# Moving copies and scalings of a mixer from VectorE to ScalarE and GpSimd in a two-layer hybrid model

## The chip, the core and the metric

The kernel runs on one core of a Trainium2 chip. The core has five engines that run beside each other and meet only at semaphores: TensorE (PE) multiplies matrices into PSUM, VectorE (DVE) and ScalarE (ACT) work elementwise on SBUF and PSUM, GpSimd (POOL) works elementwise on SBUF, and SyncE (SP) starts the transfers. Each engine takes its instructions in the order in which they stand in its queue. The metric is the device time of one execution in microseconds.

## The reference

Two layers, each made of a SwiGLU feed-forward block, a mixer, a cross attention and a second feed-forward block, with a layer norm behind each. There are 256 tokens of width 1024, everything in float32. The mixer is what matters here. It projects the tokens into a gated short convolution, a gated linear recurrence of four heads (hgrn2) and a pool over windows of 2, 4, 8 and 16 tokens:

```python
def hgrn2(q, f_logit, v, g, lb, norm_g):
    f = lb + (1.0 - lb) * jax.nn.sigmoid(f_logit.astype(f32))
    logf = jnp.log(f)
    k = 1.0 - f
    ...
        decay = jnp.exp(jnp.where(mask[:, :, None], diff, -jnp.inf))
        attn = jnp.einsum('bhtd,bhsd,bhtsd->bhts', qb, kb, decay)
        o = (jnp.einsum('bhts,bhsv->bhtv', attn, vb)
             + jnp.einsum('bhtd,bhdv->bhtv', qb * jnp.exp(b), state))
    ...
    o = o * lax.rsqrt(jnp.mean(jnp.square(o), axis=-1, keepdims=True) + RMS_EPS)
    o = o * norm_g.reshape(REC_HEADS, REC_HEAD_DIM).astype(f32)
    o = o.reshape(bsz, s, REC_DIM) * jax.nn.sigmoid(g.astype(f32))
```

The pool's group sums are multiplied by a small matrix and by a scale per channel (`y * scale`). The three results, side by side, go through `w_out`.

## The kernel before, in words

Every weight is loaded once from HBM in raw blocks of 1 MB. A helper `split` (L61, L62) turns each half of a block into two parts: ACT casts it to a rounded float (`whi`, L61), and DVE subtracts that from the raw value (`wlo`, L62). Large products run as three products of such parts (L100 to L103) and share one line, L103. PSUM tiles come from two rings of four, `acc` and `dn`; a product that needs a tile of a ring waits until the reader of the tile four places earlier is done.

A product's result leaves PSUM by two steps: ACT copies one half (L123, or L599 in the forward form used here), and DVE adds the other half to it (L124, or L600 and L601).

The mixer works on two blocks of 128 tokens. It computes the recurrence without a scan, by levels: at level c (1, 2, 4, ..., 64) the products of q and k between neighbouring blocks of c tokens are taken (L672) and written into the matrix `AT` under a mask (`copy_predicated`, L698). Between levels, q and k are multiplied in place by the decay across the block (L691 for q, L688 for k). The products at a level need the k of every second block in contiguous order, so `blocks(c)` (L657 to L663) copies them into a tile `kc`, of which there are two; the copy is on line 660 and, before, on DVE. The copy for level 2c reads what L688 of level c wrote, and L688 of level 2c writes over what the copy read.

The order of the PE in this part is written out by hand (`manual_schedule` with PE): between the products of the levels stand the projections of the values, the pool, the convolution and the gates. After the last level comes the product across the two token blocks (L715, copied out on ACT at L716). Then, for each of the two token blocks i: the products with v (L726, L727), the squares with their row sums on ACT (L731, four heads), the mean plus epsilon (L732), the power -0.5 on POOL (L733), the scaling of the result into `yr` (L734), and gate 1 + i (`gate`, with L599 to L601; every second gate is followed by the sigmoid at L612 on ACT and a scaling at L614 on DVE). Gate 3 comes after the loop. Behind it stand the pool's small product (L767) and its scaling (L770), the splits of the convolution and the pool into `xT`, the transposes of `yr` (L778), the first product with `w_out`, and, from `fill`, products of keys for the attention that do not depend on the mixer.

The order on the other engines is set by a scheduler that places the instructions when the program is built; it follows from the dependencies and the engine each instruction is on. A changed engine can therefore change the order of its neighbours.

Of the kernel before, what the change touches and what calls it, by code (L numbers as in the profile page):

```python
# [11 lines left out]
AF = mybir.ActivationFunctionType  # L12
ALU = mybir.AluOpType
# [4 lines left out]
P = 128  # L18
# [6 lines left out]
HEADS = 4  # L25
ALPHA = (2.0 * DEPTH) ** 0.25
LN_EPS = 1e-5
RMS_EPS = 1e-6
# [18 lines left out]
def model(ctx: ExitStack, tc: tile.TileContext, t: dict, out: bass.AP):  # L47
    nc = tc.nc
# [5 lines left out]
    def acc(shape=(P, 2, SEQ), tag="acc"):  # L54
        return ps.tile(list(shape), F32, tag=tag, name=tag)
# [138 lines left out]
    psc = prm[:, 28:32].rearrange("p (l j) -> p l j", l=DEPTH)  # L194
# [351 lines left out]
    def mixer(l, fill):  # L546
        w_in = t["w_in"][l]
        with tc.tile_pool(name="mix", bufs=1, reuse_waits="tile") as mp:
# [90 lines left out]
            def view(x, base, *dims, keep=False):  # L639
                return bass.AP(  # L640
                    tensor=x.tensor, offset=x.offset + base,
                    ap=[list(x.ap[0])] + [list(d) for d in dims if keep or d[1] > 1],
                )

            other = HEADS * P
            for b in range(NT):
                o = acc((P, HEADS, P), "dn")
# [9 lines left out]
            def blocks(c):  # L657

                kc = mp.tile([P, HEADS, P], F32, tag="kc", name="kc", bufs=2)
                nc.vector.tensor_copy(  # L660
                    kc.rearrange("p h (a w c) -> p w (h a) c", w=2, c=c),
                    view(kf, 0, (other + c, 2), (2 * c, HEADS * 64 // c), (1, c), keep=True),
                )  # L663
                return kc

            kc = blocks(1)
            for n, c in enumerate(LEVELS):
                a = 64 // c
                products_of_others((1, 2, 1, 2, 1, 2, 2)[n])
                o = acc((P, HEADS, NT, 64), "dn")  # L670
# [18 lines left out]
                if c < 64:  # L689
                    kc = blocks(2 * c)  # L690
# [16 lines left out]
            def gate(j, o=None):  # L707
                add_forward(sg[:, j, :], mm_cols(w_gate, slice(j * P, (j + 1) * P), xT) if o is None else o)
                if j % 2:
                    ev_g(j // 2)  # L710

            first = mm_cols(w_gate, slice(0, P), xT)
            o = acc((P, HEADS, P), "dn")
# [6 lines left out]
            yr = mp.tile([P, NT, HEADS, P], F32, tag="f", name="yr")  # L720
            for i in range(NT):
                o = acc((P, HEADS, P), "dn")
                for hh in range(HEADS):
                    c = slice(hh * P, hh * P + P)
                    if i:
                        nc.tensor.matmul(o[:, hh, :], AX_[:, hh, :], v[:, 0, c], start=True, stop=False)  # L726
                    nc.tensor.matmul(o[:, hh, :], AT[:, i, hh, :], v[:, i, c], start=i == 0, stop=True)  # L727
                ss = sm.tile([P, HEADS], F32, tag="ss", name="ss")
                jk = mp.tile([P, P], F32, tag="jk", name="jk", bufs=2)
                for hh in range(HEADS):  # L730
                    nc.scalar.activation(jk, o[:, hh, :], AF.Square, accum_out=ss[:, hh : hh + 1])  # L731
                nc.vector.tensor_scalar(ss, ss, 1.0 / P, RMS_EPS, op0=ALU.mult, op1=ALU.add)  # L732
                nc.gpsimd.tensor_tensor(ss, ss, nhalf, op=ALU.pow)  # L733
                nc.vector.tensor_tensor(yr[:, i], o, ss[:, :, None].to_broadcast([P, HEADS, P]), op=ALU.mult)  # L734
                gate(1 + i)
            gate(3)
            by_hand.__exit__(None, None, None)
# [3 lines left out]
            for g, w_ in enumerate(WINDOWS):  # L741
# [4 lines left out]
                    op=ALU.add,  # L746
                )
                pr, j = slice((g % 2) * 64, (g % 2) * 64 + 64), g // 2
# [7 lines left out]
            for j in range(2):  # L756
                nc.vector.tensor_scalar_mul(yc[:, j, :], u[:, j, 2 : 2 + SEQ], cw[:, l, 2, j : j + 1])
                for s in (1, 0):
                    nc.vector.scalar_tensor_tensor(  # L759
                        yc[:, j, :], u[:, j, s : s + SEQ], cw[:, l, s, j : j + 1], yc[:, j, :],  # L760
                        op0=ALU.mult, op1=ALU.add,
# [3 lines left out]
            o = acc()  # L765
            for j in range(2):
                nc.tensor.matmul(o[:, j, :], wpool[:, l, j, :], win[:, j, :], start=True, stop=True)  # L767
            yp = win
            for j in range(2):
                nc.vector.tensor_scalar_mul(yp[:, j, :], o[:, j, :], psc[:, l, j : j + 1])  # L770


            split(xTh[:, 0:2, :], xTl[:, 0:2, :], yc)
# [102 lines left out]
    for l in range(DEPTH):  # L876
        pend = ffn(l, "ffn1", 0, pend, early=None if l else lambda op: (load_memory(op), small_parameters(op)))
        keys(l, 0, {6: pend})
        pend = mixer(l, lambda: keys(l, 1))
        pend = attention(l, pend)  # L880
        pend = ffn(l, "ffn2", 3, pend, last=l == DEPTH - 1)
# [27 lines left out]
```

## Time and profile before

| | |
|---|---|
| median of 3 runs | 1117.33 us (1117.31 to 1117.41) |
| the profiled execution | 1118.65 us |
| its span, first to last instruction | 1116.9 us |
| granted TensorE clock, mean | 0.998 |
| PE, DVE, ACT, POOL busy | 1102.9, 822.4, 594.2, 41.8 us |
| first mixer's levels and end | about 213 to 277 us |
| second mixer's levels and end | about 763 to 827 us |

A row of a time line gives the start of an instruction from the start of the span, its length, its engine, its source line, its operation, what it writes and reads, and how many like it follow each other; in brackets stands how long the engine was idle before it and who ended that. A row of a group gives the count, the busy time, the mean length in nanoseconds and the idle time before. Several instructions on an engine overlap at their ends, so the distance between starts is shorter than a length.

### The profile page before, as it was taken

What the parts mean: (1) busy time and instruction counts of PE and PEld (TensorE: products, weight loads), DVE (VectorE), ACT (ScalarE), POOL (GpSimd) and SP (SyncE); (2) the same over time, 40 slices, a digit from 0 to 9 for tenths busy, and PEclk for the clock granted to TensorE, in tenths of its full rate; (3) what the DMA queues carried; (4) which work ended last, traced back from release to release, by engine and by line L of the source; (5) the groups of instructions that cost most, each with busy time, mean ns of one, the idle gap of its engine ahead of it and who ended that gap; (6) DMA issues with size and microseconds to landing.
All of it is one profiled execution on the core that took longest, in us unless ns stands there. A gap on an engine that the chain in (4) does not pass through costs nothing. (4 is left out here: it accounts for less than half of the span.)

```text
span 1116.9 us, 15747 instructions
## 1 busy us (share of the span) xinstructions
PE 1102.9 (99%) x6227; PEld 992.6 (89%) x6227; DVE 822.4 (74%) x1195; ACT 594.2 (53%) x873; POOL 41.8 (4%) x80
## 2 busy tenths in 40 slices
PE   9999999999999999999999999999999999999997
PEld 7989998998889889999889999889988998999996
DVE  6766677898888666666677666598988777766665
ACT  6665553645466456455355555455454653665550
POOL 7000000000000000000000000000000000000000
PEclk9999999999999999999999999999999999999999
DMA  8855565743465375656466655655445645755551
GB/s 309 301 211 202 194 221 156 240 170 139 163 243 180 105 262 191 226 204 211 151 226 234 214 182 186 237 186 194 151 146 183 237 152 164 249 189 203 181 182 38
DMA packets 98378, 218.23 MB, mean 195 GB/s; under 512 B 3776, under 2 KB 16352, under 8 KB 98304
## 3 DMA queue, kind: packets, MB, share of 16 engines
q1 hardware_dynamic: 97536, 215.89, 56.1%
q8 instruction: 49, 0.80, 0.3%
q10 hardware_dynamic: 576, 1.18, 0.3%
q14 instruction: 25, 0.20, 0.1%
q0 software_dynamic: 192, 0.15, 0.0%
HBM read 216.15 MB, written 1.05 MB: 194 GB/s over the span
## 5 line engine op out<-in xcount | busy, mean ns | idle before, releaser
L62 DVE TENSOR_TENSOR wlo<-raw,whi 128x1024 fp32r<-128x1024 f32 (+1 forms) x396 | 469.1, 1208 | 102.6 <-ACT whi L61 66.6
L61 ACT CAST whi<-raw 128x1024 fp32r<-128x1024 f32 (+1 forms) x396 | 398.2, 1041 | 170.7 <-PE dn L103 127.6
L103 PE MATMUL acc<-xT,whi 128*128 128x512 f32 x1600 | 388.3, 381 | 0.6 <-DVE xT L62 0.6
L103 PEld LDWEIGHTS acc<-xT,whi 128*128 128x128 f32 x1600 | 288.9, 190 | 33.8 <-DVE xT L62 1.1
L103 PEld LDWEIGHTS acc<-xT,wlo 128*128 128x128 f32 x1600 | 209.7, 191 | 10.8
L103 PE MATMUL acc<-xT,wlo 128*128 128x256 f32 x1600 | 210.8, 275 | 0.0
L103 PE MATMUL dn<-whi,ah 128*128 128x512 f32 x346 | 131.6, 380 | 0.0
L103 PE MATMUL dn<-wlo,ah 128*128 128x512 f32 x346 | 131.1, 379 | 0.0
L103 PE MATMUL dn<-whi,al 128*128 128x512 f32 x346 | 131.1, 379 | 0.0
L103 PE MATMUL dn<-whi,xT 128*128 128x512 f32 x288 | 88.9, 384 | 0.0
L103 PE MATMUL acc<-whi,xT 128*128 128x512 f32 x288 | 88.4, 381 | 0.0
L124 DVE TENSOR_TENSOR sg<-acc,sg 128x256 f32<-128x256 f32 x72 | 30.4, 422 | 69.7 <-ACT sg L123 69.6
L103 PEld LDWEIGHTS dn<-whi,al 128*128 128x128 f32 x346 | 65.4, 189 | 9.3
L103 PEld LDWEIGHTS dn<-wlo,ah 128*128 128x128 f32 x346 | 65.4, 189 | 9.2
L103 PEld LDWEIGHTS dn<-whi,ah 128*128 128x128 f32 x346 | 65.5, 189 | 8.6
L123 ACT COPY sg<-acc 128x256 f32<-128x256 f32 x72 | 26.7, 371 | 84.0 <-PE acc L103 83.8
L103 PEld LDWEIGHTS dn<-whi,xT 128*128 128x128 f32 x288 | 54.8, 191 | 7.5
L103 PEld LDWEIGHTS acc<-whi,xT 128*128 128x128 f32 x288 | 54.3, 189 | 7.6
L103 PE MATMUL dn<-wlo,xT 128*128 128x512 f32 x144 | 54.9, 381 | 0.0
L103 PE MATMUL acc<-wlo,xT 128*128 128x512 f32 x144 | 54.6, 379 | 0.0
L123 ACT COPY up<-acc 128x256 f32<-128x256 f32 x72 | 26.7, 370 | 49.0 <-PE acc L103 48.0
L304 POOL TENSOR_TENSOR rs<-rs,nhalf 128x1 f32<-128x1 f32 x16 | 14.9, 933 | 903.6 <-DVE rs L303 903.6
(196 smaller groups left out, 1048.5 us busy)
## 6 DMA issues: line engine op xcount, KB each, us to landing
raw<-in_ffn_up_dram SPq DMA_DIRECT2D x44, 1024.0 KB, 5.1
raw<-in_ffn_down_dram SPq DMA_DIRECT2D x44, 1024.0 KB, 4.9
raw<-in_ffn_gate_dram SPq DMA_DIRECT2D x42, 1024.0 KB, 5.0
raw<-in_w_in_dram SPq DMA_DIRECT2D x24, 1024.0 KB, 5.1
raw<-in_ca_k_dram SPq DMA_DIRECT2D x8, 1024.0 KB, 5.0
raw<-in_w_out_dram SPq DMA_DIRECT2D x8, 1024.0 KB, 4.9
raw<-in_ca_v_dram SPq DMA_DIRECT2D x8, 1024.0 KB, 6.0
raw<-in_ca_q_dram SPq DMA_DIRECT2D x8, 1024.0 KB, 5.0
```

The costliest lines, as they stand in the source:

```text
L61: nc.scalar.copy(hi, src)
L62: nc.vector.tensor_tensor(lo, src, hi.bitcast(F32), op=ALU.subtract)
L103: nc.tensor.matmul(o, w, x, start=start, stop=stop)
L123: nc.scalar.copy(dst, o[:, 1])
L124: nc.vector.tensor_tensor(dst, o[:, 0], dst, op=ALU.add)
L304: nc.gpsimd.tensor_tensor(rs, rs, nhalf[:, 0:1], op=ALU.pow)
```

## The change

Four edits, all in the mixer, none of which changes a product on the PE or a transfer:

1. The copy of the blocks of k into `kc` (seven per layer) is an ACT copy instead of a DVE copy.
2. The multiplication by 1/128 and the addition of epsilon on the sums of squares (two per layer, 128x4) is on POOL instead of DVE, directly ahead of the power that was there already.
3. The scaling of the recurrence's result into `yr` (two per layer) becomes four ACT activations each, one per head, whose scale is that head's column of `ss`.
4. The scaling of the pool's two sums (two per layer) becomes ACT activations with a column as the scale.

```diff
@@ blocks(c)
-                nc.vector.tensor_copy(
+                nc.scalar.copy(
                     kc.rearrange("p h (a w c) -> p w (h a) c", w=2, c=c),
                     view(kf, 0, (other + c, 2), (2 * c, HEADS * 64 // c), (1, c), keep=True),
                 )
@@ the loop over the token blocks
                     nc.scalar.activation(jk, o[:, hh, :], AF.Square, accum_out=ss[:, hh : hh + 1])
-                nc.vector.tensor_scalar(ss, ss, 1.0 / P, RMS_EPS, op0=ALU.mult, op1=ALU.add)
+                nc.gpsimd.tensor_scalar(ss, ss, 1.0 / P, RMS_EPS, op0=ALU.mult, op1=ALU.add)
                 nc.gpsimd.tensor_tensor(ss, ss, nhalf, op=ALU.pow)
-                nc.vector.tensor_tensor(yr[:, i], o, ss[:, :, None].to_broadcast([P, HEADS, P]), op=ALU.mult)
+                for hh in range(HEADS):
+                    nc.scalar.activation(yr[:, i, hh, :], o[:, hh, :], AF.Copy, scale=ss[:, hh : hh + 1])
                 gate(1 + i)
@@ the pool
             for j in range(2):
-                nc.vector.tensor_scalar_mul(yp[:, j, :], o[:, j, :], psc[:, l, j : j + 1])
+                nc.scalar.activation(yp[:, j, :], o[:, j, :], AF.Copy, scale=psc[:, l, j : j + 1])
```

As built, the PE's and SP's orders are the same as before. On ACT, the four scalings of token block i stand directly behind the squares of that block and ahead of the half copy of gate 1 + i; behind the second of these half copies follow two weight casts, the cast of the convolution into `xT`, the half copy of gate 3, another weight cast and the two scalings of the pool. On DVE the two weight remainders still stand between the evictions of gates 2 and 3.

## The prediction

> **What bounds the kernel now.** I read the page's head first, then the PE's waits, then three stretches of the first mixer, then the time lines of PE, DVE, ACT and POOL where the PE stands still.
>
> ```profile
> span 1116.9 us, 15747 instructions
> PE 1102.9 (99%) x6227; PEld 992.6 (89%) x6227; DVE 822.4 (74%) x1195; ACT 594.2 (53%) x873; POOL 41.8 (4%) x80
> ```
> ```profile
> PE acc L103 <- DVE sg L601: 2.4, 2, 1.2
> PE dn L389 <- DVE kTh L384: 1.5, 1, 1.5
> PE dn L715 <- DVE q L691: 1.2, 2, 0.6
> ```
> ```profile
> 222.00:261.00 39.00, 38.83 (x247) 35.67 (x245) 38.79 (x76) 16.16 (x23) 0.00 (x0) 1.00 0.47 161
> 261.00:277.00 16.00, 14.36 (x96) 13.24 (x97) 12.42 (x31) 10.21 (x29) 2.20 (x2) 1.00 0.37 132
> ```
> TensorE is busy for 99% of the span, so a change on other engines can only move its waits. In the mixer there are two kinds, once per layer: 0.6 us at L715 for the last rescaling of q on DVE, and 1.2 us at the first product of the keys behind the mixer, for the DVE copy of the last gate (L601), which frees a PSUM buffer. In the stretch of the decay's levels (222 to 261; the columns are length, PE, PEld, DVE, ACT, POOL) DVE is busy for 38.79 of 39 us and ACT for 16.16: there DVE is full. In the stretch behind it (261 to 277) DVE has 3.6 us of room: there the order of the steps decides, a chain over ACT, DVE and POOL.
>
> ```profile
> 260.44 0.38 PE L103 MATMUL acc<-xT,whi 128*128 128x512 f32 x1
> 261.43 1.16 PE L715 MATMUL dn<-q,k 128*128 128x128 f32 x8 [0.60 <-DVE q L691]
> 274.62 0.46 PE L103 MATMUL dn<-whi,xT 128*128 128x512 f32 x1
> 276.30 1.75 PE L103 MATMUL acc<-mT,whi 128*128 128x512 f32 x7 [1.21 <-DVE sg L601]
> ```
> ```profile
> 226.05 0.43 DVE L660 COPY kc<-k 128x512 f32<-128x512 f32 x1
> 243.91 0.68 DVE L691 TENSOR_TENSOR q<-q,tot 128x512 f32<-128x512 f32 x1
> 260.69 0.68 DVE L691 TENSOR_TENSOR q<-q,tot 128x512 f32<-128x512 f32 x1
> 265.81 0.16 DVE L732 TENSOR_SCALAR ss<-ss 128x4 f32<-128x4 f32 x1
> 267.26 0.69 DVE L734 TENSOR_TENSOR yr<-dn,ss 128x512 f32<-128x512 f32 x1 [0.91 <-POOL ss L733]
> 268.47 0.28 DVE L600 TENSOR_TENSOR sg<-acc,half 128x128 f32<-128x128 f32 x1
> 268.67 0.28 DVE L601 TENSOR_TENSOR sg<-acc,half 128x128 f32<-128x128 f32 x1
> 273.40 2.35 DVE L62 TENSOR_TENSOR wlo<-raw,whi 128x1024 fp32r<-128x1024 f32 x2
> 275.67 0.28 DVE L600 TENSOR_TENSOR sg<-acc,half 128x128 f32<-128x128 f32 x1
> 275.87 0.28 DVE L601 TENSOR_TENSOR sg<-acc,half 128x128 f32<-128x128 f32 x1
> ```
> ```profile
> 264.89 0.20 ACT L731 ACTIVATION_READ_ACCUMULATOR jk<-dn 128x1 f32 x1
> 268.99 0.63 ACT L612 ACTIVATE sg<-sg 128x512 f32<-128x512 f32 x1 [2.48 <-DVE sg L601]
> 269.52 0.26 ACT L731 ACTIVATE jk<-dn 128x128 f32<-128x128 f32 x1
> 270.88 0.20 ACT L731 ACTIVATION_READ_ACCUMULATOR jk<-dn 128x1 f32 x1
> 270.97 0.36 ACT L599 COPY half<-acc 128x256 f32<-128x256 f32 x1
> 271.22 2.00 ACT L61 CAST whi<-raw 128x1024 fp32r<-128x1024 f32 x2
> ```
> ```profile
> 266.04 1.19 POOL L733 TENSOR_TENSOR ss<-ss,nhalf 128x4 f32<-128x4 f32 x1 [74.28 <-DVE ss L732]
> 271.35 1.01 POOL L733 TENSOR_TENSOR ss<-ss,nhalf 128x4 f32<-128x4 f32 x1 [4.12 <-DVE ss L732]
> ```
> The reader sees the chain of now: the squares of the second row block end on ACT at 271.08, DVE and POOL make the scale by 272.36, DVE scales (0.69), evicts gate 2, makes two weight remainders (2.27) and evicts gate 3 by 276.15; the PE goes on at 276.30. ACT had long gone on meanwhile, since it did not wait for POOL: it copied gate 2 at 270.97.
>
> **The change part by part.** Prices of operations come from these rows.
>
> ```profile
> L824 ACT ACTIVATE e<-dn,mx 128x256 f32<-128x256 f32 x16 | 7.4, 472 | 5.8 <-DVE mx L820 5.8
> L123 ACT COPY sg<-acc 128x256 f32<-128x256 f32 x72 | 26.7, 371 | 84.0 <-PE acc L103 83.8
> L731 ACT ACTIVATE jk<-dn 128x128 f32<-128x128 f32 x16 | 4.4, 275 | 1.1 <-PE dn L727 0.7
> L61 ACT CAST ah<-sg 128x512 fp32r<-128x512 f32 x36 | 22.3, 620 | 45.2 <-DVE sg L460 45.2
> L304 POOL TENSOR_TENSOR rs<-rs,nhalf 128x1 f32<-128x1 f32 x16 | 14.9, 933 | 903.6 <-DVE rs L303 903.6
> L733 POOL TENSOR_TENSOR ss<-ss,nhalf 128x4 f32<-128x4 f32 x4 | 4.4, 1098 | 156.8 <-DVE ss L732 156.8
> L191 POOL MEMSET nhalf<- 128x4 f32 x1 | 0.1, 105 | 0.0
> ```
> ```profile
> L215 POOL TENSOR_SCALAR_AFFINE_SELECT mf<-mf x14: 235/524/1182, 7.4 to 19.3; 128x64 f32<-128x64 f32 x14
> L219 POOL TENSOR_SCALAR_AFFINE_SELECT mf<-mf x14: 242/404/1220, 9.2 to 19.7; 128x64 f32<-128x64 f32 x14
> ```
> ```profile
> 225.81 0.59 ACT L593 COPY v<-acc 128x512 f32<-128x512 f32 x1 [4.95 <-PE acc L103]
> 248.64 0.37 ACT L599 COPY half<-acc 128x256 f32<-128x256 f32 x1 [3.14 <-PE acc L103]
> ```
> *The copies of k.* Seven copies of 0.43 us leave DVE per layer, seven of about 0.62 us (a 128x512 cast out of SBUF) go to ACT, which is idle for more than half of that stretch. The next rescaling of k (L688) overwrites what the copy reads, so DVE now waits for ACT: 0.62 and a hop in place of 0.43, while it saves its own 0.43. DVE's last L691, at 260.69, so comes at least 0.8 us earlier if only a third of the six copies in that stretch (2.6 us) is gained, and the wait at L715 goes. The PE then starts L715 at 260.44 + 0.22 (0.22 is the spacing of such products) = 260.66 in place of 261.43: 0.77 us earlier. On ACT the casts and half copies queued behind a copy of k sit in gaps like these of 4.95 and 3.14 us. Bounds of the copy on ACT: 0.43 (as on DVE) and twice 0.62 (if strided addresses halve the rate); I take 0.62.
>
> *The scale of yr on ACT.* One DVE instruction of 0.69 becomes four activations 128x128 whose scale is a column. L824 reads such a column and takes 472 against 371 for the copy of the same size, so 0.10 more; on 275 that makes 0.375, with 0.28 from one start to the next, because activations overlap by about 0.1 (268.99 + 0.63 against 269.52). Four occupy 1.12 us (0.72 if the column were free). Above all ACT, which works in order, now stands behind POOL: the half copy of the next gate, the weight casts, the cast of the convolution into xT and the half copy of gate 3 are queued behind it.
>
> *The mean squares on POOL.* DVE's 0.16 goes, POOL gets an operation T on 128x4 and a hop to itself. No row shows this operation on POOL. Bounds: a fill of that size takes 0.105; the power of that size 1.10. The nearest kind is the select, of the scalar family, one tensor in and out, medians 0.524 and 0.404; I take T = 0.46. The select has 64 columns, which speaks for less; the power takes 0.93 even for one column, which speaks for more.
>
> [...]
>
> *The pool's two scalings.* Two activations of 0.47 replace two DVE operations of 0.47. The cast that reads them feeds a product that comes after the keys, some ten microseconds later. That cover hides them, and the half copies of the keys behind them come about 0.4 us late under products of 2.6 us: nothing. If the cover were gone, 0.8 us a layer. No DMA is added or moved in its queue; a raw weight buffer comes free some three microseconds later once, in a stretch whose DMA share is 0.37.
>
> *The sum for one layer* (hops from the rows: DVE to POOL 0.07, POOL onwards 0.03, others 0.04). First squares end at 265.09 - 0.77 = 264.32. Then 0.07 + T 0.46 + 0.07 + 1.19 + 0.03 + 1.12 = 2.94, so the half copy of gate 1 starts at 267.26 and ends at 267.63. DVE's two evictions end at 0.04 + 0.20 + 0.28 behind it, 268.15; the sigmoid starts at 268.19 (now 268.99), the second squares at 268.72 and they end 1.56 later, at 270.28 (now 271.08). Again 0.07 + 0.46 + 0.07 + 1.01 + 0.03 + 1.12 = 2.76: the half copy of gate 2 starts at 273.04 instead of 270.97. The first weight cast follows at 273.29 and ends at 274.34 (the second ends at 275.29 and the cast of the convolution behind it about 275.9, where the PE stops first, inside the same wait); DVE's two remainders start at 274.38 and take 2.27, to 276.65; gate 3 is out at 277.13 and the PE goes on at 277.28, not 276.30. So +0.98 a layer: 0.77 gained at L715 is more than given back. Two layers: +1.96 us. The profiled execution took 1118.65 us (span 1116.9), so it would take 1120.6; the median of the runs is 1.32 below it, and the same difference on 1117.33 gives 1119.3 us, +0.18%. As a formula, 0.98 + 2 (T - 0.46) per layer. What this kernel's measurement can tell from no change is about 0.2%, 2.23 us, which is reached at T = 0.53.
>
> **The rivals.** B: T costs what the power costs, 1.10; its 0.93 for one column speaks for a fixed price of arithmetic on POOL, the fill's 0.105 against it. +2.26 a layer, 1121.8 us. C: T is as short as the fill: +0.27 a layer, 1117.9. D: the copies of k hold DVE up. At 1.24 us a copy, the rescaling at 243.91, which now ends 0.29 before the PE needs it at 244.88, comes late, and so may its neighbour; it decides from about 0.9 us a copy and costs some 0.8 a layer more: 1120.9. Idle ACT and a saved 0.43 speak against it. E, faster: the wait behind the mixer goes too. Then the PE would resume 0.22 after 274.62, at 274.84, less 0.77: 2.23 a layer, 1112.9 at the floor. It decides only if gate 3 is out about 2.1 us earlier than I have it; T at the fill and a free column give 0.71 + 0.80 = 1.51, so more would have to fall away, and that is what speaks against it.
>
> **How the numbers follow.** My forecast, T between fill and power as the selects have it: 0.54; about 0.24 of it lies above T = 0.53, since one median is at 0.524, and 0.30 below. B 0.18, C 0.14, D 0.07, E 0.07. Faster is E, 0.07; within 0.2% is 0.30 + 0.14 = 0.44; slower is 0.24 + 0.18 + 0.07 = 0.49. The range goes from the fill with a free column (0.98 - 0.71 - 0.80 = -0.53 a layer, 1116.3) to B with half a microsecond for the copies, 1122.3; it leaves out E and little else. The likeliest case's own range is 1118.4 to 1120.6 (T 0.24 to 0.8).
>
> **What would show it.** Right: the wait at L715 is gone; L732 stands on POOL and L734 on ACT at about 0.375; ACT idles behind POOL twice a layer; the PE waits at the end of the mixer for ACT's cast of xT (about 1.5 us) and then for L601 (about 1.1). Wrong: T outside 0.24 to 0.8, waits at L672 for q, or PE waits at the mixer's end below 1.2 us.

## The result and the profile after

| | before | after |
|---|---|---|
| median | 1117.33 us (1117.22 to 1117.67, 21 executions) | 1118.54 us (1117.90 to 1119.91, 21 executions) |
| after by before | | 1.0014, 95% interval 1.0008 to 1.0020 |
| profiled execution, its span | 1118.65, 1116.9 us | 1119.91, 1118.2 us |
| granted clock of the profiled execution | 0.998 | 0.997 |

The median moved by +1.21 us, 0.11%: within the 0.2% that the prediction set as its bound of no change, and 0.8 us below its 1119.3. But the 21 executions after fall into two groups, twelve at 1117.9 to 1118.5 (median 1118.25) and nine at 1119.7 to 1119.9. Before, all 21 lie within half a microsecond (the profiled execution of before, 1118.65 us, is not one of them).

The waits of the PE after (releaser; total us, times, longest us):

```profile
PE dn L103 <- ACT xT L61: 2.3, 2, 1.2
PE acc L103 <- DVE sg L601: 1.9, 2, 0.9
```

The row for L715 is gone; the wait behind the mixer is now two waits in a row. The time lines of PE, POOL and ACT in the first mixer after (start, length, and in brackets the idle time and its end; from L735 on, a line number is one higher than before):

```profile
259.51 1.05 PE L715 MATMUL dn<-q,k 128*128 128x128 f32 x8
274.02 0.48 PE L103 MATMUL dn<-whi,xT 128*128 128x512 f32 x1 [1.16 <-ACT xT L61]
275.44 2.51 PE L103 MATMUL acc<-mT,whi 128*128 128x512 f32 x7 [0.94 <-DVE sg L601]
...
263.15 0.19 POOL L732 TENSOR_SCALAR ss<-ss 128x4 f32<-128x4 f32 x1 [72.68 <-ACT jk L731]
263.43 1.23 POOL L733 TENSOR_TENSOR ss<-ss,nhalf 128x4 f32<-128x4 f32 x1
268.82 0.19 POOL L732 TENSOR_SCALAR ss<-ss 128x4 f32<-128x4 f32 x1 [4.16 <-ACT jk L731]
269.10 1.02 POOL L733 TENSOR_TENSOR ss<-ss,nhalf 128x4 f32<-128x4 f32 x1
...
264.70 1.14 ACT L735 ACTIVATE yr<-dn,ss 128x128 f32<-128x128 f32 x4 [1.63 <-POOL ss L733]
270.15 1.14 ACT L735 ACTIVATE yr<-dn,ss 128x128 f32<-128x128 f32 x4 [1.42 <-POOL ss L733]
271.17 0.39 ACT L599 COPY half<-acc 128x256 f32<-128x256 f32 x1
273.31 0.65 ACT L61 CAST xT<-cv 128x512 fp32r<-128x512 f32 x1
```

The reader sees three things. L715 runs without a wait. ACT stands twice behind POOL, 1.63 and 1.42 us, and only then copies gate 2's half (271.17) and casts the convolution (273.31), for which the PE waits. And the seven products at 275.44, which took 1.75 us before, take 2.51.

The PE's order is the same before and after, so every product has its counterpart in the other trace. Set against each other in this way, three things move in each of the two layers. At one of the products of the levels (L672) the PE comes 0.13 us later. It starts L715 0.77 us earlier, reckoned from there. And it resumes behind the mixer 0.42 and 0.41 us later than before in all, reckoned from the products ahead of that L672. That is +0.83 us for both layers; the group without slow products stands +0.92 above the median of before. Between these places the two traces keep the same distance to 0.03 us, but for the products at half clock and the first 11 us. In these 11 us the kernels are the same, and still the profiled execution of before falls 1.28 us behind: its first products of 128x512 on line 103, from 7.68 to 8.52, take 0.63 us each, their counterparts after 0.38 to 0.48. So the difference of the two profiled spans does not measure the change.

The 0.13 us at L672 stand in the row of the PE's weight loads (PEld), before and then after, with the rescaling of q that comes ahead of it on DVE:

```profile
244.67 1.08 PEld L672 LDWEIGHTS dn<-q,kc 128*128 128x128 f32 x8
```
```profile
242.84 0.68 DVE L691 TENSOR_TENSOR q<-q,tot 128x512 f32<-128x512 f32 x1
243.63 0.97 PEld L672 LDWEIGHTS dn<-q,kc 128*128 128x128 f32 x8 [0.16 <-issue]
```

Before, the loads run without a gap, 0.08 us behind the end of the rescaling of q (243.91 + 0.68); after, they start 0.11 us behind its end (243.52), with a gap of 0.16. The profile names no releaser. That it is q is concluded from this: the products here come 0.08 to 0.13 us later in the trace of every kernel below that has the copies of k on ACT, and in none that has them on DVE.

The 2.51 us are the other group. The view by windows gives, for a stretch, its length, the busy time (and instructions) of PE, PEld, DVE, ACT and POOL, the granted clock, the DMA share and GB/s. After, at the end of the first and of the second mixer:

```profile
272.87:276.28 3.41, 1.32 (x5) 0.98 (x6) 3.41 (x6) 3.41 (x7) 0.00 (x0) 1.00 0.05 16
276.28:279.69 3.41, 3.41 (x14) 3.04 (x13) 3.07 (x6) 1.62 (x3) 0.00 (x0) 0.50 0.73 292
822.42:825.83 3.41, 2.26 (x16) 1.84 (x14) 2.14 (x4) 3.41 (x9) 0.00 (x0) 1.00 0.01 2
825.83:829.24 3.41, 2.47 (x14) 2.02 (x15) 3.41 (x8) 3.41 (x7) 0.00 (x0) 1.00 0.42 118
```

and before, at the end of the first:

```profile
273.23:276.64 3.41, 2.20 (x15) 1.77 (x14) 3.41 (x8) 3.14 (x5) 0.00 (x0) 1.00 0.01 2
276.64:280.05 3.41, 3.41 (x21) 3.11 (x20) 3.41 (x8) 1.65 (x5) 0.00 (x0) 1.00 0.79 304
```

These stretches are not chosen freely: the changes of the granted clock in these traces lie on a grid of 3.413 us (after, at 276.28, 279.69 and 1115.96 us, that is 1 and 245 times 3.413 apart; in the traces of runs 2 and 6 below, the half-clock stretches of the two layers start 552.96 us apart, 162 times), and the rows are cells of that grid. After, the cell with the stand-still had the PE busy for 1.32 us, and for the whole next cell the PE was granted half the clock: 3.41/2 = 1.7 us lost (1.66 by the products behind it), about the 1.6 us between the two groups. In the second layer the same stand-still lay across two cells (2.26 and 2.47 us busy) and nothing followed. Only the profiled executions show their cells; that the other executions near 1119.8 have such a cell is concluded from their time and from their lower mean clock (0.996 to 0.997 in most, 0.998 and 0.999 in the lower group).

### The profile page after: what moved, and what is told of

Same layout as the page of the kernel before. It is cut to its first block, busy times and chain, and to the rows that moved or that the text cites. A ratio compares the mean times of both kernels' runs of the same rounds, so it can differ in the third digit from the quotient of the medians.

```text
span 1118.2 us, 15773 instructions
## 1 busy us (share of the span) xinstructions
PE 1103.6 (99%) x6227; PEld 992.6 (89%) x6227; DVE 815.0 (73%) x1169; ACT 608.5 (54%) x907; POOL 45.6 (4%) x84
## 3 DMA queue, kind: packets, MB, share of 16 engines
HBM read 216.15 MB, written 1.05 MB: 194 GB/s over the span
## 4 chain that ended last, share of the span: by engine, by line
PE 91%; DVE 5%; ACT 1%; issue 1%; POOL 0%; DMA 0%; DVEq 0%; SPq 0%
PE acc L103 60%; PE dn L103 28%; DVE wlo L62 2%; PE dn L672 1%; PE acc L167 1%; ACT jk L731 1%; DVE h L311 1%; DMA raw<-in_ffn_gate_dram 0%; DVE xT L62 0%; ACT whi L61 0%; POOL ss L733 0%; DVE h L297 0%; ACT yr L735 0%; DVE h L307 0%; PE dn L649 0%
```

## The experiments

Theory: the price of the change is that ACT's queue (the next gate's half copy, the casts) stands behind POOL's two steps and the scalings, twice a layer; the k copies pay part of it back; and a longer stand-still of the PE costs half the clock in the cell behind it, if it falls into one cell. Rivals: the parts' prices are those of their instructions, wherever they stand; the two groups have another cause than the stand-still. Line numbers in a kernel with added lines are its own.

**1. The copies of k alone.**

```diff
 (the kernel before)
-                nc.vector.tensor_copy(
+                nc.scalar.copy(
                     kc.rearrange("p h (a w c) -> p w (h a) c", w=2, c=c),
```

> The kernel before with one part of the change: the seven copies of k per layer are on ACT. Theory (my chain): VectorE is full at 222 to 261 us, so the wait at L715 goes (-0.77 us a layer), and the small steps behind the levels start without a queue, so the end of the mixer comes earlier too: squares 0 end 264.3, scale of yr done 266.2, squares 1 end 268.8, gate 3 out about 274.3 instead of 276.15, -1.9 a layer in all. Time 1113.6 us (1113 to 1114.5), ratio 0.9967, PE wait at the mixer's end below 0.7 us. Rival 1 (only the wait at L715 goes, the chain at the end only shifts with it): 1115.8 us. Rival 2 (the end of the mixer is bound elsewhere and takes the gain back): 1117.3 us, the wait at the end grows to 2.0.

Measured: 1114.85 us, 0.9977 (0.9968 to 0.9986). The L715 wait is gone and the end wait is 0.8 us in place of 1.2: so the time lies between the theory's 1113.6 and the rival's 1115.8. Where the missing 1.2 us went, from DVE's and POOL's time lines of this kernel:

```profile
262.21 1.39 DVE L759 SCALAR_TENSOR_TENSOR cv<-u,prm,cv 128x256 f32<-128x256 f32 x3
263.51 0.16 DVE L732 TENSOR_SCALAR ss<-ss 128x4 f32<-128x4 f32 x1
...
263.75 1.45 POOL L733 TENSOR_TENSOR ss<-ss,nhalf 128x4 f32<-128x4 f32 x1 [73.42 <-DVE ss L732]
268.72 1.01 POOL L733 TENSOR_TENSOR ss<-ss,nhalf 128x4 f32<-128x4 f32 x1 [3.52 <-DVE ss L732]
```

The squares end at 262.88, but DVE works off three steps of the convolution before it comes to the mean at 263.51; and the power beside DVE takes 1.45 us, against 1.01 where DVE is idle. A freed DVE fills up with other steps of the queue.

**2. The scalings alone.**

```diff
 (the kernel before)
-                nc.vector.tensor_tensor(yr[:, i], o, ss[:, :, None].to_broadcast([P, HEADS, P]), op=ALU.mult)
+                for hh in range(HEADS):
+                    nc.scalar.activation(yr[:, i, hh, :], o[:, hh, :], AF.Copy, scale=ss[:, hh : hh + 1])
```

> The kernel before with one part of the change: the scaling into yr is four ACT activations per token block. Theory (ACT stands behind GpSimd, and the half copies of gates 1 and 2 and the weight casts stand behind it): the wait at L715 stays at 0.6; the half copy of gate 2 starts 2.5 to 2.9 us later, gate 3 is out 1.6 to 1.8 us later; time 1120.4 us (1120 to 1121) when the clock stays up, and in some executions about 1.6 to 1.7 us more, as in the changed kernel, since the PE stands still for over 2 us at the mixer's end. Rival (this part is neutral and the cost of the change is elsewhere): 1117.3, same waits as before.

Measured: 1123.86 us, 1.0053 (1.0040 to 1.0066); two executions at 1122.2, three at 1123.9 to 1124.2. In the profiled one both layers have a half-clock cell (below), and without them each layer is 1.63 us longer, so +3.3, 1120.5 with the clock's part taken off: the expected 1120.4. The clock's part comes on top, once or twice 1.65 us.

**3. The mean step alone.**

```diff
 (the kernel before)
-                nc.vector.tensor_scalar(ss, ss, 1.0 / P, RMS_EPS, op0=ALU.mult, op1=ALU.add)
+                nc.gpsimd.tensor_scalar(ss, ss, 1.0 / P, RMS_EPS, op0=ALU.mult, op1=ALU.add)
```

> The kernel before with one part of the change: mean and epsilon on GpSimd (0.19 us by the trace of the changed kernel, 0.28 to the start of the power) instead of VectorE (0.16 and a hop of 0.07). Theory: for the first token block 0.4 us are gained, because VectorE's queue (0.7 us) is left out, for the second 0.05 to 0.1 are lost; the time is 1116.6 to 1117.4. Rival (GpSimd's step costs about half a microsecond, twice a layer, as I predicted it): 1118.5 or more.

Measured: 1118.12 us, 1.0008 (0.9999 to 1.0017). Neither: +0.85. POOL's and DVE's time lines of this kernel:

```profile
263.71 0.77 POOL L732 TENSOR_SCALAR ss<-ss 128x4 f32<-128x4 f32 x1 [73.40 <-ACT jk L731]
270.04 0.19 POOL L732 TENSOR_SCALAR ss<-ss 128x4 f32<-128x4 f32 x1 [4.45 <-ACT jk L731]
...
263.15 1.27 DVE L759 SCALAR_TENSOR_TENSOR cv<-u,prm,cv 128x256 f32<-128x256 f32 x3
265.62 0.69 DVE L734 TENSOR_TENSOR yr<-dn,ss 128x512 f32<-128x512 f32 x1 [1.20 <-POOL ss L733]
266.23 0.48 DVE L759 SCALAR_TENSOR_TENSOR cv<-u,prm,cv 128x256 f32<-128x256 f32 x1
```

The same instruction takes 0.19 us with DVE idle and 0.77 beside DVE's steps; it ends at 264.48, 0.06 behind the end of DVE's three steps on line 759 (264.42). And the scheduler put the scaling ahead of the last steps of the convolution, so that DVE stands for 1.20 us and then still has them to do.

**4. The pool's scale alone.**

```diff
 (the kernel before)
-                nc.vector.tensor_scalar_mul(yp[:, j, :], o[:, j, :], psc[:, l, j : j + 1])
+                nc.scalar.activation(yp[:, j, :], o[:, j, :], AF.Copy, scale=psc[:, l, j : j + 1])
```

> The kernel before, with only the pool's scale on ACT. Theory (in the kernel before these two DVE steps come behind the sg step that ends TensorE's wait, and no one waits for them there): 1117.3 us, 1117.0 to 1117.7. Rival (they hold the split of xT behind them, DVE's 0.86 us of them is on the path): 0.3 to 1 us faster.

Measured: 1117.40 us against 1117.23 beside it, 1.0000 (0.9991 to 1.0009). It costs nothing there.

The four parts alone, without the clock's share, sum to -2.4 + 3.3 + 0.85 + 0 = +1.75 us; together they make +0.9. So I put each of the first three back into the changed kernel.

**5. The changed kernel, scalings back on DVE.**

```diff
-                for hh in range(HEADS):
-                    nc.scalar.activation(yr[:, i, hh, :], o[:, hh, :], AF.Copy, scale=ss[:, hh : hh + 1])
+                nc.vector.tensor_tensor(yr[:, i], o, ss[:, :, None].to_broadcast([P, HEADS, P]), op=ALU.mult)
```

> The changed kernel, with the scaling of the recurrence back on DVE as one step of 128x512; the copies of k on ACT, the mean square on GpSimd and the pool's scale on ACT stay. Theory (the parts add: the k copies alone gave -2.4 us, the mean step alone +0.85): 1115.7 us, no stretch at half clock, so that the scalings on ACT are worth +2.5 us of the changed kernel without its clock drops. Rival (the parts interact: with the k copies off DVE the mean step costs nothing): 1114.9 or below.

Measured: 1114.81 us, 0.9977 (0.9968 to 0.9986): the rival's side. The scalings are worth 1118.25 - 1114.81 = 3.4 us of the changed kernel, about as much as alone (3.3); the mean step then costs nothing beside the k copies.

**6. The changed kernel, k copies back on DVE.**

```diff
-                nc.scalar.copy(
+                nc.vector.tensor_copy(
                     kc.rearrange("p h (a w c) -> p w (h a) c", w=2, c=c),
```

> The changed kernel, with the copies of the blocks of k back on DVE. Theory (the parts add: the k copies alone gave -2.4 us, and the changed kernel's executions without a drop of the clock stand at 1118.2): 1120.6 us without a drop, of which 1.5 us is the wait at L715 that comes back; the stand-still at the mixer's end stays about 2.1 us or grows, and where the emptiest 3.413-us stretch of the clock's grid has TensorE busy for less than about 1.6 us, the next one is granted 0.5, so that some executions stand at 1122.2. Rival (the k copies pay only through L715): 1119.7 without a drop.

Measured: 1125.59 us, 1.0076 (1.0063 to 1.0089); the profiled execution, 1125.18, has a half-clock cell in both layers, so about 1121.9 without. The k copies are worth some 3.7 us here, not 2.4. DVE's and POOL's time lines of this kernel show the other part:

```profile
263.07 1.66 DVE L760 SCALAR_TENSOR_TENSOR cv<-u,prm,cv 128x256 f32<-128x256 f32 x4
264.77 0.69 DVE L764 TENSOR_TENSOR cv<-cv,cv 128x512 f32<-128x512 f32 x1
...
263.63 1.16 POOL L732 TENSOR_SCALAR ss<-ss 128x4 f32<-128x4 f32 x1 [73.38 <-ACT jk L731]
264.88 1.47 POOL L733 TENSOR_TENSOR ss<-ss,nhalf 128x4 f32<-128x4 f32 x1
```

With DVE later by the seven copies, its steps of the convolution fall on POOL's: the mean takes 1.16 us (it ends at 264.79, 0.06 behind DVE's four steps) and the power 1.47, against 0.19 and 1.23 in the changed kernel. That is 1.2 us a layer, beside the 0.6 us wait at L715, which is back.

**7. The changed kernel, mean step back on DVE.**

```diff
-                nc.gpsimd.tensor_scalar(ss, ss, 1.0 / P, RMS_EPS, op0=ALU.mult, op1=ALU.add)
+                nc.vector.tensor_scalar(ss, ss, 1.0 / P, RMS_EPS, op0=ALU.mult, op1=ALU.add)
```

> The changed kernel, with the mean-square step back on DVE. Theory (on DVE the step stands behind cv steps that are queued ahead of it, as with the k copies alone, where it ended about 0.6 us behind the squares): about +0.3 us a layer, 1118.8 us, with drops in some executions. Rival (the mean step on GpSimd is a cost by itself, +0.85 us as it was alone): 1117.4.

Measured: 1121.30 us, 1.0039 (1.0025 to 1.0053): three executions at 1121.0 to 1121.3 and two at 1122.5. With one half-clock cell of 1.65 us taken off the first, 1119.5: the mean on POOL is a gain of about 1.3 us in the changed kernel, where alone it is a loss of 0.85. The theory's sign and twice its size (0.3 us a layer, 0.6 in all); the rival, 1117.4, is out.

**8. The mean step twice.**

```diff
 (the changed kernel)
                 nc.gpsimd.tensor_scalar(ss, ss, 1.0 / P, RMS_EPS, op0=ALU.mult, op1=ALU.add)
+                nc.gpsimd.tensor_scalar(ss, ss, 1.0, 0.0, op0=ALU.mult, op1=ALU.add)
```

> The changed kernel, with a second GpSimd step behind the mean step (times 1, plus 0), so that the two steps ahead of the power take about twice 0.28 us from start to start. Theory (GpSimd's step is on the path twice a layer, as the prediction's sum has it: 2 us of end for 1 us of step): +0.56 us a layer, 1119.3 us without a drop, and since TensorE then stands longer, a stretch at half clock in more executions and perhaps in both layers: 1121 or 1122.6 for those. Rival (the step's length is hidden): 1118.2 to 1118.5.

Measured: 1122.06 us, 1.0045 (1.0033 to 1.0058): three at 1121.8 to 1122.1, two at 1123.2 and 1123.6. Less one or two half-clock cells this is 1120.3; by the traces +1.01 and +0.99 us a layer over the changed kernel, not +0.56. POOL's time line of this kernel, first half:

```profile
262.91 0.20 POOL L732 TENSOR_SCALAR ss<-ss 128x4 f32<-128x4 f32 x1 [72.67 <-ACT jk L731]
263.18 0.40 POOL L733 TENSOR_SCALAR ss<-ss 128x4 f32<-128x4 f32 x1
263.66 1.47 POOL L734 TENSOR_TENSOR ss<-ss,nhalf 128x4 f32<-128x4 f32 x1
```

From the start of the mean to the scalings it is 2.26 us, 0.71 more than the 1.55 of the changed kernel, since the added step took 0.40 and the power 1.47 beside DVE; in the second half 1.61 against 1.33, 0.28 more. The sum, 0.99 us, is what the end moved (1.01 and 0.99). So POOL is on the path one for one, and what was wrong is the length of a POOL step.

**9. The scalings behind the next gate's half copy.**

```diff
 (the changed kernel)
-                for hh in range(HEADS):
-                    nc.scalar.activation(yr[:, i, hh, :], o[:, hh, :], AF.Copy, scale=ss[:, hh : hh + 1])
-                gate(1 + i)
+                half = gate(1 + i)
+                with tc.issue_after(half.ins):
+                    for hh in range(HEADS):
+                        nc.scalar.activation(yr[:, i, hh, :], o[:, hh, :], AF.Copy, scale=ss[:, hh : hh + 1])
```

(`gate` and the helper it calls hand back the half copy's instruction.)

> The changed kernel, with ACT's four scalings of the recurrence issued behind the half copy of the next gate, not ahead of it. Theory (in the changed kernel the price of the scalings on ACT is that two gates' half copies and sigmoids, and behind them the cast of xT and the third gate's half copy, stand behind GpSimd's two steps and the four scalings): the third half copy and the sg step behind it come 0.9 to 1.2 us earlier in each layer, TensorE's wait at the mixer's end falls from about 2.1 us to about 1, no stretch at half clock follows: 1115.6 us, 1114.8 to 1116.5. Rival (it is DVE or the casts, not ACT's order, that set the end): no earlier, 1118.2, and some executions still near 1119.8.

Measured: 1114.50 us, 0.9974 (0.9964 to 0.9984), 3.75 us below the changed kernel's group without half clock, a little under the range. ACT's and PE's time lines of this kernel:

```profile
263.96 0.37 ACT L599 COPY half<-acc 128x256 f32<-128x256 f32 x1 [1.05 <-PE acc L103]
264.54 0.88 ACT L739 ACTIVATE yr<-dn,ss 128x128 f32<-128x128 f32 x3 [0.20 <-POOL ss L735]
266.07 0.29 ACT L733 ACTIVATE jk<-dn 128x128 f32<-128x128 f32 x1
...
273.70 1.78 PE L103 MATMUL acc<-mT,whi 128*128 128x512 f32 x7 [0.58 <-ACT win L774]
```

ACT waits 1.05 us for the gate's product, copies its half and then waits 0.20 us for POOL, in place of 1.63 us for POOL alone; the second squares start at 266.07 instead of 267.19, and the PE resumes at 273.70 instead of 275.44 (0.13 us of these differences lies ahead of the mixer). The same work on the same engines, in another order, is worth the whole loss and the k copies' gain besides.

**10. The same, with the mean step back on DVE.** (The edits of 9 and of 7 together.)

> The changed kernel, with the scalings of the recurrence behind the next gate's half copy on ACT and the mean-square step back on DVE. Theory (on DVE the step stands behind 0.6 us of cv steps in the first half of the tokens; now only the scalings wait for it, not the gate): 1114.5 to 1115.4, at most half of the 1.3 us that the same move back cost with the gates behind the scalings. Rival (the mean step on DVE costs as much in either order): 1115.8.

Measured: 1115.75 us, 0.9986 (0.9978 to 0.9995): the rival. The mean on DVE costs 1.25 us in this order too, as much as in 7. So the order of 9 does not take the chain of mean, power and scalings off the path; it only takes the half copy out from behind it.

**11. The order of 9, with the pool's scale back on DVE.** (The edit of 9, and the inverse of the edit of 4.)

> The changed kernel, with the scalings of the recurrence behind the next gate's half copy on ACT and the pool's scale back on DVE. With the gates first, TensorE's last wait of the mixer was for ACT's pool scale (0.58 us), which stands behind two casts and a half copy. Theory (that wait is the price of the pool's scale on ACT): it goes, and the sg step behind it or the casts of the weights are late by less: 1113.6 to 1114.2. Rival (DVE's first scale stands behind the split of xT and its second behind the sg step, so that the bank comes free no earlier): 1114.5 to 1115.2.

Measured: 1114.44 us, 0.9975 (0.9965 to 0.9985), between the two expectations and 0.06 us from 9. The PE's wait for the pool's scale is gone, and in its place it waits 0.4 us a layer for L601 and does one product of the keys earlier: one late reader took the place of another.

**12. The stand-still filled.** Sixteen transposes more per layer, which write the same values again, behind the mixer's last transposes; nothing else of the changed kernel is touched.

```diff
 (the changed kernel)
                 for hh in range(HEADS):
                     nc.tensor.transpose(pt[:, hh, :], yr[:, i, hh, :], jdn if i else idn)
+                for _ in range(4 * i):
+                    for hh in range(HEADS):
+                        nc.tensor.transpose(pt[:, hh, :], yr[:, i, hh, :], jdn)
```

> The changed kernel with sixteen more transposes per layer that write the same values again behind the last transposes of the mixer (0.11 us each, 1.8 us of PE work inside the 2.1 us for which the PE stands still there). Theory (two groups of times, 1118.2 and 1119.8, are made by the PE's clock, which drops to half for 3.4 us in some executions because of that stand-still): time 1118.2 to 1118.8 in every execution, spread below 0.7 us, granted clock 0.998 or more in each, no row of times near 1119.8. Rival (the two groups come from something else, such as transfers): both groups stay.

Measured: 1118.53 us, 1.0011 (1.0003 to 1.0020), eleven executions from 1118.35 to 1118.92, none near 1119.8. The PE's time line of this kernel:

```profile
272.52 1.91 PE L782 MATMUL acc<-jdn,yr 128*128 128x128 f32 x16
275.28 1.75 PE L103 MATMUL acc<-mT,whi 128*128 128x512 f32 x7 [0.85 <-DVE sg L601]
```

More work on the PE and the upper group is gone: the seven products take 1.75 us again. The PE resumes as late as before the filling, and the median stands 0.28 us above the lower group. So what the upper group paid was how empty the cell was, not how late the PE resumed.

**The cells of all traces.** The view by windows, for the end of a mixer, of the scalings alone (first row and the cell behind it), of the mean back on DVE (first layer, then second with the cell behind it) and of the mean step alone:

```profile
827.44:830.85 3.41, 1.58 (x6) 1.21 (x7) 3.41 (x7) 3.41 (x7) 0.00 (x0) 1.00 0.16 25
830.85:834.26 3.41, 3.41 (x14) 3.07 (x13) 2.55 (x6) 0.71 (x3) 0.00 (x0) 0.50 0.74 287
```
```profile
273.92:277.34 3.42, 1.74 (x7) 1.34 (x8) 3.42 (x6) 3.42 (x8) 0.00 (x0) 1.00 0.16 26
277.34:280.75 3.41, 3.41 (x24) 3.14 (x23) 3.41 (x8) 2.79 (x5) 0.00 (x0) 1.00 0.71 281
823.47:826.88 3.41, 1.27 (x6) 0.80 (x7) 3.07 (x5) 3.41 (x7) 0.00 (x0) 1.00 0.01 5
826.88:830.29 3.41, 3.41 (x10) 2.78 (x10) 3.41 (x7) 2.30 (x4) 0.00 (x0) 0.50 0.80 276
```
```profile
272.59:276.00 3.41, 1.76 (x13) 1.41 (x12) 3.41 (x7) 2.93 (x6) 0.00 (x0) 1.00 0.07 11
```

| emptiest cell at a mixer's end: PE busy, us of 3.41 | next cell's clock |
|---|---|
| 1.11, 1.25 (mean twice); 1.27 (mean back, second layer); 1.30, 1.50 (k copies back); 1.32 (changed kernel, first layer); 1.46, 1.58 (scalings alone) | 0.5 |
| 1.74 (mean back, first layer); 1.76 (mean alone); 2.20 (before); 2.26 (changed kernel, second layer); 2.50 (run 10); 2.56 (run 12); 2.64 (k copies alone); 2.65 (scalings back); 2.83 (run 9) | 1.0 |

Between 1.58 and 1.74 us of 3.41, about half, lies the bound, in every cell within the work. One cell at the end of a program does not fit, in the kernel with the pool's scale alone: the PE was busy for 1.47 us there and the clock stayed at 1.00 in the next, where the PE had nothing more to do. So busy time as the view counts it may not be quite what the clock goes by; this stays open.

```profile
1107.14:1110.55 3.41, 1.47 (x14) 1.28 (x12) 2.18 (x6) 0.00 (x0) 0.39 (x1) 1.00 0.00 0
```

The bound also gives the share of the executions. The changed kernel's stand-still lasts from 272.86 to 275.44, 2.58 us, of which 2.10 idle. A cell has to hold about 1.75 us of idle time, so it may miss 0.35 us at either end: its start has 3.41 - 2.58 + 2 x 0.35 = 1.53 us of room out of 3.41, 45%, if executions start anywhere on the grid. Nine of 21 are 43%. This is an estimate for one layer. The second stand-still lies 549.98 us behind the first where no half-clock cell has come between (551.64 in the profiled execution, less 1.66), and 161 cells are 549.55 us, so it stands 0.43 us later on the grid. With both layers the estimate is (1.53 + 0.43)/3.41, 57%. Nine of 21 do not tell these two estimates apart; they show no more than that the size is right.

## Why the prediction came out as it did

The time, 1118.54 us, lies in the range and on the side the prediction gave 0.44; its own likeliest value was 0.8 us too high. Two errors stand against each other: a term too large by 1.1 us, and a mechanism that it did not have, the clock, which adds 1.6 us to nine executions and 0.29 us to the median. That the median fell into the lower group is luck: had two more of the 21 executions met the half-clock cell, it would be 1119.7. And of the prediction's own signs of being wrong, one came up (T below 0.24) and another did in small (a wait at L672).

- *The copies of k and L715.* Right: the wait is gone, 0.77 us a layer by the sum, 0.77 measured. The copy was taken at 0.62 us; the rows below have 0.624 as the median. Rival D came up in small, at the place that it named, at 0.13 us a layer in place of 0.8. The prediction counted 0.29 us from the end of the rescaling of q to the product at 244.88; but the weight load of that product starts at 244.67, 0.08 us behind that end, so there was less room than it thought.
- *The scalings.* Taken 0.375 us each, measured 0.367. That ACT stands behind POOL with the half copies and casts queued behind it is the main step, and it held: the scalings put back (5), and the order turned (9), each take more than the whole loss away. The two waits that the PE has now, for ACT's cast and then for L601, are those the prediction named, about 1.5 and 1.1 us, measured 1.16 and 0.94.
- *T, the mean on POOL.* The mis-sized term: "medians 0.524 and 0.404; I take T = 0.46". It took 0.192 us in all four places, outside the 0.24 to 0.8 beyond which the prediction called itself wrong. The select was no kin of this operation. The fill of that size, 0.105 us, which the prediction had as its lower bound, was nearer. In the prediction's formula, 0.98 + 2 x (0.19 - 0.46) = +0.44 a layer, 1118.2 us: the lower group of executions, 1118.25, between the forecast and its rival C (1117.9). By the traces it is +0.42 and +0.41, but in part by other terms: 0.13 of it is the wait at L672, and against that stand, among others, eight products at L715 that take 1.05 us in place of 1.16, and four scalings that occupy 1.02 us (270.15 to 271.17) in place of 1.12.
- *The pool's scalings* at nothing: right; 0.515 us each against 0.47 taken, and nothing on the time of the kernel (4 and 11).
- *The granted clock.* No step and no rival had it. The prediction let the PE's stand-still cost what it lasts; it cost 1.7 us more where a cell of 3.41 us held 1.58 us of work or less. Nine of 21 executions paid that; without them the median would be 1118.25.

The groups of these instructions after, by line (count; shortest, median and longest in ns; first and last start; shapes):

```profile
L732 POOL TENSOR_SCALAR ss<-ss x4: 192/192/193, 263.2 to 820.5; 128x4 f32<-128x4 f32 x4
L735 ACT ACTIVATE yr<-dn,ss x16: 359/367/377, 264.7 to 822.6; 128x128 f32<-128x128 f32 x16
L771 ACT ACTIVATE win<-acc,prm x4: 514/515/517, 275.0 to 827.1; 128x256 f32<-128x256 f32 x4
L660 ACT COPY kc<-k x14: 617/624/833, 211.4 to 796.5; 128x512 f32<-128x512 f32 x14
```

Two things stay open: the exact place of the clock's bound between 1.58 and 1.74 us, with the one cell that does not fit it, and what holds the load at L672, since the profile does not name it.

The kernels of 1, 5, 9, 10 and 11 are faster than both, by 0.1 to 0.3% of the time before. The best two, 9 and 11, stand at 0.9974 and 0.9975 of before, and their intervals overlap with those of 1 and 5: moving the k copies alone gives nearly all of the gain.

## What to carry to other kernels

Before a step is moved to an engine that works in order, look at what is queued behind it there: the same scalings cost 3.4 us ahead of the next gate's half copy and nothing behind it (1114.50 us, against 1114.81 with them on VectorE). Price a small GpSimd step twice, once with VectorE idle and once beside its steps (0.19 and 0.77 us for the same instruction in run 3), and see which of the two the new order gives it. And look at how empty a stand-still of TensorE leaves a cell of the clock's grid: with 1.58 us of work or less in 3.41, the next 3.41 us were granted 0.50 here (but for the one cell at a program's end in run 4), which added 1.6 us to nine of 21 executions; work in the gap took that away (1.9 us of transposes in run 12, at 0.28 us over the lower group).

## What the runs showed of the hardware that was not expected

- *Half the clock behind a cell that still held work.* Cells with 1.11 to 1.58 us of work in 3.413 us were followed by 3.413 us at 0.50, cells with 1.74 us and more were not; the cell at the end of run 4, with 1.47 us, was not either. So cells that were from a third to nearly half work (1.11 and 1.58 of 3.413 us) were empty enough. The changes lie on one grid of 3.413 us (276.28, 279.69 and 1115.96 us in the changed kernel).
- *GpSimd beside VectorE.* One 128x4 step took 0.19, 0.40, 0.77 or 1.16 us, and the power of that size 1.01 to 1.47. With VectorE idle the step took 0.19 us (268.82 in the changed kernel, 270.04 in run 3) and the power 1.01 or 1.02 (268.72 in run 1, 269.10 in the changed kernel). In run 3 the step started at 263.71, within VectorE's three steps on line 759 (263.15 to 264.42), and ended 0.06 us behind the last of them; in run 6 it started at 263.63, within four of them (263.07 to 264.73), and again ended 0.06 us behind the last; so did the second step of run 8 (0.40 us, from 263.18). In runs 3 and 6 the step lasted not only through the VectorE step that was running but through those that followed it too. The time lies inside the GpSimd instruction and not in a wait ahead of it; that the two engines met here at something other than a semaphore is concluded from these ends, and the profile does not name it. In the changed kernel the step took 0.19 us although it stood at 263.15 among three such VectorE steps: the second and the third of them start 0.53 us apart, the first and the second 0.39, so here VectorE seems to have been the one that was held, by 0.14 us. The prediction took one length for a GpSimd step everywhere. The mean step was worth +0.85 us alone and -1.3 us in the changed kernel; its length is one cause of that, and what VectorE's queue did around it is the other (runs 3 and 7).

DVE's time line of the changed kernel around POOL's step at 263.15, the three steps in one row and then the second and the third by themselves:

```profile
262.37 1.42 DVE L760 SCALAR_TENSOR_TENSOR cv<-u,prm,cv 128x256 f32<-128x256 f32 x3
```
```profile
262.76 0.50 DVE L760 SCALAR_TENSOR_TENSOR cv<-u,prm,cv 128x256 f32<-128x256 f32 x1
263.29 0.49 DVE L760 SCALAR_TENSOR_TENSOR cv<-u,prm,cv 128x256 f32<-128x256 f32 x1
```
